# Slots 4 and 5 interleaved by the halves of w, one piece of w settled on another engine, and new engine orders for slots 0 to 25

## The chip, the cores and the metric

One core of a Trainium2 chip runs the whole kernel. The metric is the time of one execution in device microseconds. A profiled execution gives a page and a trace besides; its times are microseconds from the start of its span.

## The reference

```python
xw = x @ w                                   # x: 16 x 2048 x 1024, w: 1024 x 1024
out[:, 0, :] = xw[:, 0, :]
for t in range(1, S):                        # S = 2048
    out[:, t, :] = decay[None, :] * out[:, t - 1, :] + xw[:, t, :]
```

A dense matrix product, and behind it a first-order recurrence along time, of its own decay for each of the 1024 columns.

## The kernel before

**Tiles and slots.** Time is cut into 64 chunks of 512 steps, and two chunks of one batch make a group. The 1024 output columns are cut into 8 parts n of 128. One tile is a group by a part: 128 columns on the partitions, 1024 steps along the free side. TensorE works tile by tile in *slots*: slot s is the s-th tile, so slots 0 to 7 are chunks 0 and 1, slots 8 to 15 are chunks 2 and 3, and so on. A tile takes 16 matmuls of 512 columns (8 blocks k of w's rows by two chunks). Slots 0 to 3 are computed together, with their chunks in pieces, while x and w still arrive; slots 8 and 9 are also computed together.

**How x comes.** Each chunk is read by four DMAs (`load`, L105) of 256 KB that GpSimd issues and that turn float32 into bfloat16, into one of three buffers `xb`. VectorE transposes the chunk in 32x32 blocks into one of two buffers `xw` (`turn`, L115, called T), and ScalarE copies that in two halves into one of five buffers `xt` (`part`, L123, called X and Y), which TensorE reads. When T of chunk c is recorded, the four loads of chunk c+3 join a list; each L in an order takes the next load from that list.

**How w comes.** w lies in four staging quarters: half h of the columns by even or odd rows e. `settle` (L326) turns one piece m of a quarter into bfloat16 in `wsb`. Pieces are numbered i = 8h + 4e + m, so pieces 8 to 11 are the third quarter (even rows of the second half of the columns, which slots 4 to 7 need) and 12 to 15 the fourth (its odd rows). `W` settles on VectorE and `w` on ScalarE. `r` makes GpSimd copy one element of a settled piece (L376), so that what stands behind it on GpSimd waits for that piece.

**The recurrence.** Tiles whose n is 3 or 7 are scanned by VectorE out of PSUM (S at L229). The others are *paired*: ScalarE copies the tile out of PSUM (p, L191) and multiplies the even steps by the decay (g, L171); GpSimd adds these to the odd steps (j, L205); VectorE scans the odd steps alone, half as many (S at L210); ScalarE multiplies (h, L171) and GpSimd adds (c, L266) to fill in the even steps. z sets the element before the first (L199, L201) and k keeps the last (L270). `flips` turns the kind of some tiles over: tile 1 is scanned whole, so is tile 13. At last VectorE transposes a tile back (B, L278) into one of four buffers `ot`; when four tiles are there, SyncE issues four DMAs of 512 KB to the output (L302).

**PSUM.** Tiles rotate over three buffers `ps`. Slot 4 takes that of tile 0, slot 5 that of tile 1, and, farther on, slot 22 that of tile 19 and slot 26 that of tile 23. TensorE may start a tile only when the tile before it in the buffer has been read: by p and g where it is paired, by S where it is not.

**What sets the order.** Nothing is scheduled by the compiler: `pin` keeps the order in which the code records instructions, engine by engine. A table by hand, `agenda`, lists for each slot what is recorded behind its matmuls, for slots 0 to 33 and the last 20; the slots between follow the rule `usual`. An order says nothing of when: each engine runs its own list in order, waiting by semaphores for what it needs. Only the order within one engine counts, so a deed may stand under a later slot and still come at the same place of its engine's list.

Of the kernel before, what the change touches and what calls it, by code (L numbers as in the profile page):

```python
# [10 lines left out]
BF16 = mybir.dt.bfloat16  # L11
# [14 lines left out]
def kernel(  # L26
# [34 lines left out]
    K = CQ // P  # L61
    M = K // 2
    TL = 512
    NJ = TL // P
    NC = S // TL
    R = K // 2
# [3 lines left out]
    const = ctx.enter_context(tc.tile_pool(name="const", bufs=1))  # L70
    sb = ctx.enter_context(tc.tile_pool(name="sb", bufs=1))
    psp = ctx.enter_context(tc.tile_pool(name="psp", bufs=1, space=bass.MemoryType.PSUM))
# [3 lines left out]
    def ring(pool, name, count, shape, dtype=FP32):  # L76
        i = turns[name] = turns.get(name, -1) + 1
        return pool.tile(shape, dtype, name=f"{name}{i % count}")
# [20 lines left out]
    xt_of = {}  # L99
# [25 lines left out]
    def matmul(ps, n, k, xt, t0=0, t1=TL, start=0, pairs=None):  # L125
        if pairs is None:
            rhs = xt[:, k // 2, k % 2, t0:t1]
        else:
            rhs = pairs[:, k // 2, t0 // P:t1 // P, :, k % 2].rearrange("p j i -> p (j i)")
        lhs = wsb[:, k, n].rearrange("p q i -> p (q i)")  # L130
        return pin(nc.tensor.matmul(  # L131
            out=ps[:, t0 % ps.shape[1]:][:, 0:t1 - t0],
            lhsT=lhs,
            rhs=rhs,
            start=(k == 0 and t0 == start),
            stop=(k == K - 1),
        ))
# [233 lines left out]
        settle(i // 8, i // 4 % 2, i % 4, copy)  # L371

    def await_settled(i):
        mark = const.tile([128, 1], BF16, name="mark")
        h, e, m = i // 8, i // 4 % 2, i % 4
        pin(nc.gpsimd.tensor_copy(out=mark, in_=wsb[:, 2 * m + e, h * R, 0, 0:1]))  # L376

# [35 lines left out]
    def finale():  # L413
        six, six_late = ring(psp, "ps", 3, [128, TL]), ring(psp, "ps", 3, [128, TL])
        seven, seven_late = ring(psp, "spare", 1, [128, TL]), ring(psp, "ps", 3, [128, 2 * TL])
        return ((six[:, 0:TL // 2], six_late[:, TL // 2:TL]),
                (seven[:, 0:TL // 2], (seven_late[:, 0:TL // 4], seven_late[:, TL:TL * 5 // 4])))

    def half_of(n, half, ks=range(K)):
        ps = finals[n % R - 2][half]  # L420
        t = half * (TL // 2)
        for k in ks:
            matmul(ps, n, k, xt_of[nch - 1], t, t + TL // 2, t)
# [60 lines left out]
    def turn_and_load(c):  # L484
# [42 lines left out]
    }  # L527
    agenda = {
        -99: "M0 U0 M1 M2 M3 U1 U2 w0 W1 w2 W3 K3 E0 E1 G0 E2 G1 E3 F2 G3 W4 w5 W6 W7 D E4 E5 G4 E6 G5 E7 F6 G7 E8 E9 G8 E10 G9 E11 F10 G11 E12 L E13 G12 L E14 G13 E15 L F14 G15",
        0: "p0 z0",  # L530
        1: "g0 S1 w8 w9 w10 w11",
        2: "L L",
        3: "p2 z2 L W12 W13 W14 W15 g2 r15 j0 S3 k1",
        4: "j2 B1 d k3 L L",
        5: "p4 S0 g4 S2 k0 h0 j4 L L B3 h2",
        6: "k2 c0 T2 c2 L p5 g5 B0 L X2 L",
        7: "B2 L L Y2 T3 L z4 z5 j5 p6 S4 z6 L g6 L X3 S5 j6 S7 Y3 L S6 h4 k7 k5 c4 k4 h5 B7",
        8: "",
        9: "k6 h6 c5 B4",
        10: "p8 g8 c6 T4 z8 p9 j8 g9 B5 X4",  # L540
        11: "L j9 B6 p10 S8 L z9 z10 g10 S9 h8",
        12: "j10 Y4 S11 L c8 h9 T5 c9",
        13: "p12 L g12 B9 j12 X5 S10 L",
        14: "Y5 B8 L B11 h10 z12 c10 S13",
        15: "p14 L g14 S12 j14 T6 h12 L",
        16: "p15 c12 g15 B10 L X6 j15 B12",
        17: "z14 Y6 S14 L B13 z15 h14 S15 p16 z16 c14",
        18: "g16 T7 L h15 j16 p17 g17 B14 z17 c15 X7",
        19: "S16 j17 p18 B15 L g18 L S17 k16 h16 z18 j18",
        20: "Y7 S19 L c16 k17 h17 T8 k19 L c17",  # L550
        21: "p20 g20 L S18 X8 j20 B17 B19",
        22: "L h18 p21 c18 B16 k18 g21 B18 Y8 z20 L j21 S20",
        23: "p22 z21 z22 S21 L h20 g22 T9 c20 h21",
        24: "k21 k20 j22 S23 X9 L c21 Y9 B20 L",
        25: "B23 k23 p24 B21 g24 z24 j24 S22 z25",
        26: "p25 T10 k22 h22 g25 c22 S24 X10 j25",
        27: "B22 p26 S25 g26 z26 Y10 j26",
        28: "S27 h25 h24 c25 S26 c24",
# [36 lines left out]
    def usual(s):  # L595
        paired = [t.paired for t in tiles]
        do = [f"P{s}"] if paired[s] else []
        if paired[s - 1]:
            do.append(f"S{s - 1}")
        if not paired[s]:  # L600
            do.append(f"S{s}")
        do.append(f"C{s - 1}")
        if paired[s - 2]:
            do.append(f"B{s - 2}")
        if not paired[s - 1]:
            do.append(f"B{s - 1}")
        return do + later.get(s, []) + ["L"] * (2 if len(loads) > NQ else 1)
# [8 lines left out]
    def perform(do):  # L616
        for deed in do:
            deeds[deed[0]](int(deed[1:] or 0))
# [3 lines left out]
    for step, (g, n) in enumerate(slots):  # L622
        T = TL * len(g)
        left = step - len(slots)
        if n % R == 0:
            ns, nj = range(n, n + R), T // P
            if left == -2 * R:
                outlets = [Outlet(ns, H, half) for half in range(2)]
            else:
                pieces = 1 if left < -7 * R else 2 if left < -6 * R else nj // H  # L630
                outlets = [Outlet(ns, nj, pieces=pieces)]
        if left == -R:
            outlets = []
        if step == 0:
            heads = [ring(psp, "ps", 3, [128, T]) for _ in range(3)]
            firsts = [ps[:, 0:TL] for ps in heads] + [spares[0]]
            seconds = [ps[:, TL:T] for ps in heads] + [spares[1]]
            for j0, j1 in cuts[0]:
                for e in range(2):
                    for k in range(e, K, 2):  # L640
                        for i in range(R):
                            matmul(firsts[i], i, k, xt_of[0], j0 * P, j1 * P, j0 * P,
                                   pairs=None if e else xw_of[0])
            Q = cuts[1][0][1] * P
            for k0 in range(0, K, 2):
                for i in range(R):
                    for k in (k0, k0 + 1):
                        matmul(seconds[i], i, k, xt_of[1], 0, Q,
                               pairs=xw_of[1] if k0 < 4 else None)
            for i in range(R):  # L650
                for k in range(K):
                    matmul(seconds[i], i, k, xt_of[1], Q, TL, Q,
                           pairs=xw_of[1] if i < 2 else None)
        if step < R:
            ps = heads[n] if n < 3 else tuple(spares)
        else:
            if step == K + 1:
                ps = nexts
            elif left >= -2:
                finals = finals if left == -1 else finale()  # L660
                ps = finals[left + 2]
            elif len(g) == 2 or n % R < 3:
                ps = ring(psp, "ps", 3, [128, T])
            else:
                ps = ring(psp, "spare", 1, [128, TL])
            todo = [(k, l) for k in range(K) for l in range(len(g))]
            if step < K:
                todo.sort(key=lambda kl: kl[0] % 2)
            elif step == K:
                todo = []  # L670
                nexts = (ring(psp, "spare", 1, [128, TL]), ring(psp, "ps", 3, [128, T])[:, TL:T])
                for l in range(len(g)):
                    for i, one in enumerate((ps[:, l * TL:(l + 1) * TL], nexts[l])):
                        for k in range(K):
                            matmul(one, n + i, k, xt_of.get(g[l]),
                                   pairs=xw_of[g[l]] if l or not i and k >= M else None)
            elif step == K + 1:
                todo = []
            if left == -2:
                for m, half in ((n, 0), (n + 1, 0), (n, 1)):  # L680
                    half_of(m, half)
            if left >= -2:
                todo = []
            if 40 <= step < 180:
                pin(nc.tensor.nop(hint="room", nofuse=True))
            for k, l in todo:
                matmul(ps[:, l * TL:(l + 1) * TL], n, k, xt_of[g[l]])
        tiles.append(Tile(g, n, ps, outlets))
        do = agenda.get(step, agenda.get(left) if left >= -20 else None)
        if do is None:  # L690
            do = usual(step)
        else:
            do = do.split()
            if left == -20:
                do = rest(step) + do
        perform(do)
# [29 lines left out]
```

## Time and profile before

| | |
|---|---|
| median of 3 runs (lowest, highest) | 903.59 us (903.53, 903.96) |
| the profiled execution's own time | 905.63 us |
| its span | 903.8 us |
| TensorE busy | 890.3 us, 99% |
| VectorE, ScalarE, GpSimd busy | 825.1, 686.1, 656.5 us |
| granted TensorE clock, mean of the core | 1.0 |
| DMA | 204.77 MB, mean 227 GB/s |

The profiled execution is 1.8 us longer than its span, and 2.0 us over the median of the runs without a profile. Busy time of TensorE is modelled from matmuls that overlap: a matmul of 512 columns is shown with some 0.38 us, while starts lie 0.216 us apart. A few per cent of the matmul records are missing.

### The profile page before, as it was taken

Reading aid. Unit: us, or ns where it says so; the run is one execution under the profiler, and the core shown is the slowest. Engines: PE = TensorE matmul, PEld = TensorE weight load, DVE = VectorE, ACT = ScalarE, POOL = GpSimd, SP = SyncE. Lnnn points to the kernel's source line nnn. Section 1 sums busy time; section 2 is a strip of 40 time slices with the busy share of each in tenths; the row PEclk is TensorE's granted clock in tenths of the full one; section 3 lists DMA queues with packets and bytes.
Section 4 is the critical chain, followed back from the end, with each engine's and each line's share of the span. In section 5 each row is a group of like instructions: output and inputs, shape, how many; then the busy total and the mean of one; then the engine's idle time right before and its main releaser. Section 6 shows DMA issues by size and latency. Waiting matters only on the chain.

```text
span 903.8 us, 12213 instructions
## 1 busy us (share of the span) xinstructions
PE 890.3 (99%) x4130; PEld 412.7 (46%) x4211; DVE 825.1 (91%) x632; ACT 686.1 (76%) x958; POOL 656.5 (73%) x757
## 2 busy tenths in 40 slices
PE   7999999999999999999999999999999999999997
PEld 5544444444444444444444444444444444444444
DVE  4999998998999999999998999999999999999998
ACT  3899968877877877778778778777787787787743
POOL 7978679777767777777677687777777776876632
PEclk9999999999999999999999999999999999999999
DMA  9999999999999999999999999999999999999868
GB/s 185 176 215 215 219 245 213 215 231 255 249 245 257 254 253 249 251 247 234 224 233 228 223 232 226 233 225 227 231 231 226 229 236 222 226 228 215 180 148 229
DMA packets 403182, 204.77 MB, mean 227 GB/s; under 512 B 9392, under 2 KB 402096, under 8 KB 403120
## 3 DMA queue, kind: packets, MB, share of 16 engines
q1 hardware_dynamic: 265808, 134.77, 61.0%
q0 software_dynamic: 137024, 68.70, 56.3%
q8 instruction: 33, 0.54, 0.2%
q10 hardware_dynamic: 288, 0.52, 0.2%
q14 instruction: 29, 0.24, 0.1%
HBM read 138.42 MB, written 134.22 MB: 302 GB/s over the span
## 4 chain that ended last, share of the span: by engine, by line
PE 97%; DMA 1%; issue 1%; POOL 0%; DVE 0%; DVEq 0%; POOLq 0%
PE ps L131 96%; DMA xb<-in_x_dram 1%; PE spare L131 1%; POOL xb L105 0%; PE spare L410 0%; PE ps L410 0%; DVE h L438 0%; DVE xw L115 0%; DVEq L721 0%; DVEq L115 0%; POOLq L710 0%
## 5 line engine op out<-in xcount | busy, mean ns | idle before, releaser
L131 PE MATMUL ps<-xt,wsb 128*128 128x512 bf16 (+1 forms) x3959 | 861.6, 377 | 4.3
L131 PEld LDWEIGHTS <-wsb 128*128 128x128 bf16 x4184 | 408.2, 98 | 477.8 <-issue 1.0
L205 POOL TENSOR_TENSOR xs<-h,xs 128x512 f32<-128x512 f32 (+1 forms) x190 | 242.6, 1277 | 187.5 <-ACT h L171 84.8
L278 DVE STREAM_TRANSPOSE ot<-so 128x1024 f32<-128x1024 f32 (+2 forms) x264 | 300.4, 1176 | 5.1 <-DMA out_dram<-ot 2.5
L191 ACT COPY xs<-ps 128x1024 f32<-128x1024 f32 (+1 forms) x190 | 188.9, 994 | 152.1 <-PE ps L131 140.7
L266 POOL TENSOR_TENSOR so<-h,xs 128x512 f32<-128x512 f32 (+1 forms) x189 | 240.5, 1274 | 41.7 <-ACT h L171 25.7
L123 ACT COPY xt<-xw 128x2048 bf16<-128x2048 bf16 (+3 forms) x136 | 242.3, 1790 | 8.2 <-DVE xw L115 8.2
L105 POOL DMA_DIRECT2D xb<-in_x_dram x264 | 173.8, 659 | 5.2 <-DMA xb<-in_x_dram 3.6
L171 ACT ACTIVATE h<-so,dec 128x512 f32<-128x512 f32 (+1 forms) x189 | 144.8, 767 | 27.9 <-DVE so L210 24.6
L115 DVE STREAM_TRANSPOSE xw<-xb 128x2048 f32<-128x2048 f32 (+3 forms) x78 | 147.3, 1900 | 7.5 <-DMA xb<-in_x_dram 7.5
L210 DVE TENSOR_TENSOR_SCAN so<-spare,keep,xs 128x512 f32<-128x512 f32 (+1 forms) x97 | 119.8, 1238 | 26.4 <-POOL xs L205 26.2
L210 DVE TENSOR_TENSOR_SCAN so<-spare,xs 128x512 f32<-128x512 f32 x93 | 113.3, 1219 | 25.6 <-POOL xs L205 22.7
L171 ACT ACTIVATE h<-ps,dec 128x512 f32<-128x512 f32 (+1 forms) x190 | 129.9, 684 | 0.0
L229 DVE TENSOR_TENSOR_SCAN so<-dec,ps 128x1024 f32<-128x1024 f32 x34 | 76.9, 2262 | 2.4 <-PE ps L131 1.6
L229 DVE TENSOR_TENSOR_SCAN so<-dec,keep,ps 128x1024 f32<-128x1024 f32 (+2 forms) x35 | 75.4, 2154 | 0.0
L270 ACT COPY keep<-so 128x1 f32<-128x1 f32 x136 | 25.5, 190 | 9.1 <-DVE so L229 8.7
L201 ACT COPY so<-keep 128x1 f32<-128x1 f32 x97 | 18.5, 191 | 2.5 <-DVE ot L278 2.3
L131 PE MATMUL ps<-xw,wsb 128*128 128x256 bf16 (+3 forms) x72 | 12.2, 306 | 0.6 <-DVE xw L115 0.6
L131 PE MATMUL spare<-xt,wsb 128*128 128x512 bf16 (+3 forms) x60 | 12.6, 329 | 0.0
L199 POOL MEMSET so<- 128x1 f32 x93 | 10.7, 116 | 0.6 <-DVE ot L278 0.6
L345 PE MATMUL spare<-wide,seed 128*128 128x512 f32 x10 | 7.3, 905 | 3.2 <-ACT seed L338 3.2
L319 POOL DMA_DIRECT2D ot<-in_w_dram x12 | 6.5, 544 | 1.8 <-DMA xb<-in_x_dram 0.9
(43 smaller groups left out, 38.0 us busy)
## 6 DMA issues: line engine op xcount, KB each, us to landing
out_dram<-ot SPq DMA_DIRECT2D x236, 512.0 KB, 10.8
xb<-in_x_dram POOLq DMA_DIRECT2D x248, 256.0 KB, 7.8
out_dram<-ot SPq DMA_DIRECT2D x56, 128.0 KB, 2.7
out_dram<-ot SPq DMA_DIRECT2D x8, 256.0 KB, 4.5
ot<-in_w_dram POOLq DMA_DIRECT2D x12, 128.0 KB, 5.2
xb<-in_x_dram POOLq DMA_DIRECT2D x8, 128.0 KB, 5.5
out_dram<-xb SPq DMA_DIRECT2D x3, 256.0 KB
xb<-in_x_dram POOLq DMA_DIRECT2D x4, 160.0 KB, 7.4
```

Source lines behind the costliest of these rows:

```text
L105: pin(nc.gpsimd.dma_start(out=xb_of[c][quad(q), j0:j1], in_=_ap(x, [[D, P], [P * D, j1 - j0], [1, CQ]], (b * S + t0 + j0 * P) * D + q * CQ)))
L115: pin(nc.vector.transpose(out=dst.rearrange("p (m j i) -> p j m i", m=M, i=P)[:, j0:j1, m0:m1], in_=src.rearrange("p (j m c) -> p j m c", ...
L123: pin(copy(out=xt_of[c][:, m0:m1, :, j0 * P:j1 * P], in_=src))
L131: return pin(nc.tensor.matmul(out=ps[:, t0 % ps.shape[1]:][:, 0:t1 - t0], lhsT=lhs, rhs=rhs, start=(k == 0 and t0 == start), stop=(k == K ...
L171: pin(nc.scalar.activation(out=h[:, i * size:(i + 1) * size], in_=src, func=mybir.ActivationFunctionType.Copy, scale=dec[:, self.n:self.n ...
L191: pin(nc.scalar.copy(out=self.xs[:, i * size:(i + 1) * size], in_=ps))
L205: pin(nc.gpsimd.tensor_tensor(out=odds, in0=self.g, in1=odds, op=ALU.add))
L210: pin(nc.vector.tensor_tensor_scan(out=so[:, 3:T + 2:2], data0=squares[-1][:, n:n + 1].to_broadcast([128, T // 2]), data1=self.xs[:, 1:T:2 ...
L229: return pin(nc.vector.tensor_tensor_scan(out=so[:, t + 2:t + 2 + size], data0=dec[:, n:n + 1].to_broadcast([128, size]), data1=ps, initia ...
L266: pin(nc.gpsimd.tensor_tensor(out=self.so[:, 2:T + 2:2], in0=self.h, in1=self.xs[:, 0:T:2], op=ALU.add))
L270: pin(nc.scalar.copy(out=self.keep, in_=self.so[:, self.T + 1:self.T + 2]))
L278: pin(nc.vector.transpose(out=outlet.ot[:, :, c0:c0 + P], in_=self.so[:, 2 + t0:2 + t0 + nj * P].rearrange("p (i t) -> p i t", t=P)))
```

## The change

The 32 matmuls of slots 4 and 5 are recorded in a new order. Before, slot 4's even row blocks, slot 4's odd ones, slot 5's even ones, slot 5's odd ones; after, slot 4 even, slot 5 even, slot 4 odd, slot 5 odd. Piece 8 of w is settled by VectorE instead of ScalarE, as the first thing behind slots 0 to 3's inputs. A second `r` (r8) makes GpSimd wait for that piece, beside the one for piece 15, and each has an element of its own to write. The agenda of slots 0 to 25 is rewritten; it holds the same deeds otherwise. From slot 26 on nothing is changed.

```diff
-        mark = const.tile([128, 1], BF16, name="mark")
+        mark = const.tile([128, 1], BF16, name=f"mark{i}")
...
-        0: "p0 z0",
-        1: "g0 S1 w8 w9 w10 w11",
-        2: "L L",
-        3: "p2 z2 L W12 W13 W14 W15 g2 r15 j0 S3 k1",
-        4: "j2 B1 d k3 L L",
-        5: "p4 S0 g4 S2 k0 h0 j4 L L B3 h2",
-        6: "k2 c0 T2 c2 L p5 g5 B0 L X2 L",
-        7: "B2 L L Y2 T3 L z4 z5 j5 p6 S4 z6 L g6 L X3 S5 j6 S7 Y3 L S6 h4 k7 k5 c4 k4 h5 B7",
-        8: "",
-        9: "k6 h6 c5 B4",
-        10: "p8 g8 c6 T4 z8 p9 j8 g9 B5 X4",
-        11: "L j9 B6 p10 S8 L z9 z10 g10 S9 h8",
...
-        17: "z14 Y6 S14 L B13 z15 h14 S15 p16 z16 c14",
-        18: "g16 T7 L h15 j16 p17 g17 B14 z17 c15 X7",
-        19: "S16 j17 p18 B15 L g18 L S17 k16 h16 z18 j18",
-        20: "Y7 S19 L c16 k17 h17 T8 k19 L c17",
-        21: "p20 g20 L S18 X8 j20 B17 B19",
-        22: "L h18 p21 c18 B16 k18 g21 B18 Y8 z20 L j21 S20",
-        23: "p22 z21 z22 S21 L h20 g22 T9 c20 h21",
-        24: "k21 k20 j22 S23 X9 L c21 Y9 B20 L",
-        25: "B23 k23 p24 B21 g24 z24 j24 S22 z25",
+        0: "",
+        1: "",
+        2: "",
+        3: "W8 L p0 g0 w9 S1 w10 W12 W13 W14 W15 w11 r8 z2 p2 k1 L g2 L S3 d r15 j0 B1 j2 S0 L k3 L",
+        4: "",
+        5: "z0 p4 L g4 S2 h0 T2 B3 h2",
+        6: "c0 k0 B0 p5 c2 g5 z5 j4 X2 T3 p6 j5 Y2 S4 L g6",
+        7: "L X3 L S5 S7 k2 L L z4 L h4 j6 c4 B2",
         8: "",
+        9: "Y3 B7 k7 p8 S6 z6",
+        10: "L g8 h5",
+        11: "c5 h6 B4 j8 T4 k5 k4 c6 p9 S8 z8 g9 p10 h8 g10 L j9 X4 L k6 B5 L B6 z10",
...
+        17: "g15 z15 j14 j15 p16 T6 B12 g16 S14 L X6 S15 h14 Y6 T7 j16 c14 h15 S16",
+        18: "L p17 g17 c15 p18 B13 B15 z16 h16",
+        19: "j17 k16 z17 L c16 g18 L B14 Y7 S17",
+        20: "j18 L h17 L S19 z18",
+        21: "X7 T8 p20 g20 k19 k17 L S18 L c17 j20 B16 X8 p21 L z20 L L B17",
+        22: "g21 h18 Y8 S20 j21 c18 h20",
+        23: "p22 z21 k18 T9 S21 g22 c20 h21 Y9 B19",
+        24: "",
+        25: "p24 B18 g24 S23 k21 B20 k20 X9 k23 j22 c21 B21 z24 B23 L L z22 j24 z25 S22",
...
             if step == K + 1:
                 ps = nexts
+            elif step == R + 1:
+                ps = fives
...
-            if step < K:
+            if step == R:
+                todo = []
+                fives = ring(psp, "ps", 3, [128, T])
+                for e in range(2):
+                    for i, one in enumerate((ps, fives)):
+                        for k in range(e, K, 2):
+                            for l in range(len(g)):
+                                matmul(one[:, l * TL:(l + 1) * TL], n + i, k, xt_of[g[l]])
+            elif step == R + 1:
+                todo = []
+            elif step < K:
                 todo.sort(key=lambda kl: kl[0] % 2)
```

The rows of slots 12 to 16 are left out here; they too are rewritten.

## The prediction

> **What bounds the kernel now.** I read the page first, then TensorE's waits, then the transfers of the stretch that the new orders cover, then VectorE and GpSimd there, in order of time. The page's first line and TensorE's list of waits:
>
> ```profile
> PE 890.3 (99%) x4130; PEld 412.7 (46%) x4211; DVE 825.1 (91%) x632; ACT 686.1 (76%) x958; POOL 656.5 (73%) x757
> ```
> ```profile
> PE spare L345 <- ACT seed L338: 3.2, 1, 3.2
> PE spare L345 <- ACT gate L361: 0.8, 1, 0.8
> PE ps L131 <- DVE xw L115: 0.6, 1, 0.6
> ```
>
> TensorE waits three times, the last time at 19.58 us, before slot 4, and the diff touches nothing ahead of slot 4. From there on the starts of its matmuls lie 0.216 us apart (0.227 where they read `xw`), and gaps are whole multiples of 0.216, which are missing records. So the changed stretch has no wait to remove: the change can gain about nothing, and costs whatever wait it brings. Behind TensorE stand the transfers. Their view from 57 to 111 us:
>
> ```profile
> GB/s 216 214 214 216 215 214 216 214 215 214 215 219 212 216 214 215 214 215 215 214 215 215 214 215 216 215 215 214 216 215 214 219 212 215 215 215 215 214 215 215
> q0 software_dynamic: 11561, 5.74, 76.9%
> q1 hardware_dynamic: 11561, 5.83, 52.7%
> out_dram<-ot SPq DMA_DIRECT2D x12, 512.0 KB, 18.2
> xb<-in_x_dram POOLq DMA_DIRECT2D x19, 256.0 KB, 12.9
> ```
>
> Flat at 215 GB/s, half of it loads: 5.74 MB in 54 us are 21.9 loads of 262,144 bytes, one each 2.46 us, and the landing events stand 2.46 us apart from 52.4 to 111.5 us. Here loads can't be hurried; a gap in their queue is not made good. VectorE in the same stretch, and GpSimd before it:
>
> ```profile
> 89.31 4.59 DVE L278 STREAM_TRANSPOSE ot<-so 128x1024 f32<-128x1024 f32 x4
> 93.82 2.49 DVE L210 TENSOR_TENSOR_SCAN so<-spare,xs 128x512 f32<-128x512 f32 x2
> 96.22 2.29 DVE L115 STREAM_TRANSPOSE xw<-xb 128x2048 f32<-128x2048 f32 x1
> 98.43 2.25 DVE L229 TENSOR_TENSOR_SCAN so<-dec,ps 128x1024 f32<-128x1024 f32 x1
> ```
> ```profile
> 41.59 1.31 POOL L205 TENSOR_TENSOR xs<-h,xs 128x512 f32<-128x512 f32 x1
> 42.84 0.10 POOL L199 MEMSET so<- 128x1 f32 x1
> 42.88 1.30 POOL L105 DMA_DIRECT2D xb<-in_x_dram  x2
> ```
>
> The turn at 96.22 is T9, the scan behind it S23, which frees the PSUM of slot 26; it ends at 100.68. Slot 26 starts at 47.62 (slot 10) + 16 x 3.453 = 102.87, so S23 has 2.2 us to spare. VectorE has no wait from 60 us to here: chunk 9 landed at 94.23, before its turn. The issue at 42.88 is the first load of chunk 6.
>
> **The change part by part.**
>
> *Slots 4 and 5.* The same 32 matmuls: 0. Odd pieces of w are needed at 26.70 + 16 x 0.216 = 30.15 instead of 28.42; they are there from 27.62 to 28.23 now, so no wait goes. Tile 5's PSUM is needed at 28.42 instead of 30.15; S1, which frees it, ends at 27.44: hidden by 1.0 us. Tile 4 is whole after 24 matmuls, at 31.9 instead of 30.15; tile 5 at 33.6 as before.
>
> *Piece 8.* On VectorE a piece costs 0.20 us, on ScalarE 0.52. Its quarter lands at 24.28, VectorE has done it by 24.6, and S1 starts at 25.15 as now, since TensorE releases it: 0, at worst 0.3 if that cover were gone. ScalarE's three other pieces are ready 0.52 earlier. r8 is one copy on GpSimd (0.19 us), waiting to about 24.65; the loads of chunk 3 behind it were issued at 25.66 and aren't later.
>
> *Early deadlines* (starts by the ScalarE chain below): X2 ends at 39.1, needed at 40.51; Y2 at 41.8, needed at 43.1. No wait, with 1.3 us in hand.
>
> *Chunk 6's first load.* This is where I find the price. In the new order of GpSimd this load stands behind c0, c2, j4, j5, j6, c4, c5, j8 and c6. By rows of the waits before (start to start): p 0.90, g 0.58, h 0.68 (0.78 when its end is waited for), X or Y 1.80, k 0.09, j or c 1.25. p4 starts at 32.1; p4, g4, h0 end at 34.4; c0 ends at 35.65, and p5, which reuses its buffer, starts at 35.7. From there ScalarE runs p5 g5 X2 p6 Y2 g6 X3 k2 h4 Y3 k7 p8 g8 h5 without a wait: 0.90 + 0.58 + 1.80 + 0.90 + 1.80 + 0.58 + 1.80 + 0.09 + 0.68 + 1.80 + 0.09 + 0.90 + 0.58 + 0.78 = 13.3, so h5 ends at 49.0. Then GpSimd's c5, j8, c6 take 3.75: the load is issued at 52.75 instead of 42.88. Chunk 5's last load lands at about 54 to 55, so the queue runs dry. What a load costs from issue to landing in a dry queue is shown by two answers, without stores (28 to 40 us) and with them (195 to 260 us):
>
> ```profile
> xb<-in_x_dram POOLq DMA_DIRECT2D x8, 256.0 KB, 6.4
> ```
> ```profile
> xb<-in_x_dram POOLq DMA_DIRECT2D x19, 256.0 KB, 7.8
> ```
>
> The least in the second stretch is 7.1. Stores run from 46 us in the new order, so I take 7.5: landing at 60.25 instead of 57.33. Bounds: 4.6 (the shortest without stores) and 8.6 (the longest with them).
>
> The Trainium skill (DMA: Bandwidth & Descriptors, Anatomy of one DMA — SWDGE (gpsimd) path) gives such a DMA about 2.0 us fixed plus its bytes at 436 GB/s, by which 256 KB would be an estimated 2.6 us, the load would follow chunk 5 at once, and the sum below would be 0. The rows above say otherwise.
>
> *From there to TensorE.* Chunk 7 is complete 7 x 2.46 later, at 77.5, and VectorE, there at 75.4, waits for it at T7. Behind it stand S16, three B, S17, S19, T8, S18, two B, S20: 2.20 + 1.12 + 3.38 + 1.12 + 2.20 + 2.20 + 1.12 + 2.25 + 1.12 = 16.7, so T9 is reached at 94.2. Chunk 9 is complete at 60.25 + 15 x 2.46 = 97.15: VectorE waits 3 us. Behind T9 now stand S21, B19 and B18 ahead of S23: 97.2 + 2.2 + 1.12 + 2.25 + 2.25 = 105.05. TensorE, due at 102.87, waits 2.2 us; with the signals 2.3. Queued behind T9 on VectorE are also the back transposes of tiles 20 to 23, whose stores have buffers to spare; and behind slot 26 everything is TensorE's and shifts with it. Nothing gives the 2.3 us back, since TensorE has no other wait.
>
> With the bounds of the latency the wait is 0 to 3.4. ScalarE's p26, p28 and p30 follow with little in hand once VectorE is late (I count some 0.2 to 0.3 us): none to 0.5 us more; I take none.
>
> **Sum.** The profiled execution would have a span of 903.8 + 2.3 = 906.1 and a time of 907.9; the runs without a profile lie 2.0 lower, so the median goes from 903.59 to 905.9 us, 0.26% up. About 0.2% (1.8 us) is what a measurement of this kernel can tell from no change.
>
> **Rivals.**
>
> *The load comes in time: no change (0.31).* The place is chunk 6's first load, the price 0 to 1.7 us, so 903.6 to 905.3. It decides at a landing of 59.7: if the load is issued before 52.2 or its latency is under 7.0, the wait falls under 1.8; at 57.9 or sooner it is nil, since T9 is then reached at about the time its chunk lands. For it: the issue time is a sum of some twenty durations, and the margin is 0.5 us; without stores 4.6 to 6.6 us were seen in a short queue. Against it: with stores, no row is under 7.1.
>
> *A gain (0.03).* TensorE would have to lose a wait of 1.8 us behind slot 4, and has none. Only the start-up differs from run to run; 901.5 would need that.
>
> *The wait cools the clock (0.04).* TensorE's first spin matmuls start 0.853 us apart for 5.3 us and then 0.43 apart: the array starts at half speed. A wait of 0.8 us at 11.3 was followed at full speed; none of 2.3 us is in the trace. If 2.3 us halved the clock for 5.3 us again, 12 matmuls would take 5.3 us instead of 2.65: 2.65 more, 908.5. The Trainium skill (TensorE: Matmul & The Clock Gate, What's actually happening) says that a whole idle window of about 3.4 us brings the half clock back; by that rule 2.3 us does not, and a second mishap is needed.
>
> *The orders change nothing on the engines:* excluded, the two programs' instruction lists differ engine by engine as told.
>
> **How the numbers follow.** Likeliest: slower by the 2.3 us wait, 905.9, with its own range 905.4 to 907.5; 0.62; with the clock's case slower in all 0.66, no change 0.31, faster 0.03. The range runs from 903.4 (load in time) to 908.5 (the clock).
>
> **What would show it.** In the changed kernel's profile: a line PE ps L131 <- DVE so L229 of 2 to 2.5 us near 102.9, once; waits of VectorE's turns for `xb` at about 75 and 94; the first load of chunk 6 issued near 52.8, landing near 60.3, and the loads behind it 2.46 apart to 114; no wait of TensorE from 19.6 to 100. I am wrong if TensorE has no wait, if it waits elsewhere (slots 8 to 10 for X2 or Y2, or behind slot 26 for ScalarE), or if loads run faster than one in 2.46 us.

## The result

| | before | after |
|---|---|---|
| median (lowest to highest, 6 runs each) | 903.78 us (903.53 to 904.34) | 907.73 us (907.45 to 908.55) |
| ratio of the runs, 95% interval | 1 | 1.0044 (1.0032 to 1.0057) |
| profiled execution, its own time / span | 905.63 / 903.8 us | 907.71 / 905.9 us |
| granted TensorE clock, mean of the core | 1.0 | 0.998 in all six runs |

The change makes the kernel 0.44% slower, 3.95 us. TensorE's busy time and its list of waits in the changed kernel (total, times, longest):

```profile
PE 896.1 (99%) x4211; PEld 412.9 (46%) x4211; DVE 825.7 (91%) x633; ACT 686.1 (76%) x957; POOL 657.0 (73%) x758
```
```profile
PE spare L345 <- ACT seed L338: 3.2, 1, 3.2
PE ps L131 <- DVE so L229: 2.9, 1, 2.9
```

The second wait is the new one: once, for a scan of VectorE out of PSUM. (A busy sum of 896.1 instead of 890.3 says little: here no matmul record is missing, before 81 were.) The timeline of VectorE around it shows whose wait it passes on, and TensorE's shows where it ends:

```profile
76.59 2.31 DVE L115 STREAM_TRANSPOSE xw<-xb 128x2048 f32<-128x2048 f32 x1 [2.40 <-DMA xb<-in_x_dram]
...
96.27 2.31 DVE L115 STREAM_TRANSPOSE xw<-xb 128x2048 f32<-128x2048 f32 x1 [2.91 <-DMA xb<-in_x_dram]
98.50 1.19 DVE L210 TENSOR_TENSOR_SCAN so<-spare,xs 128x512 f32<-128x512 f32 x1
99.61 2.33 DVE L278 STREAM_TRANSPOSE ot<-so 128x1024 f32<-128x1024 f32 x2
101.87 2.25 DVE L229 TENSOR_TENSOR_SCAN so<-dec,ps 128x1024 f32<-128x1024 f32 x1
```
```profile
104.17 36.16 PE L131 MATMUL ps<-xt,wsb 128*128 128x512 bf16 x159 [2.85 <-DVE so L229]
```

The two turns are T7 and T9, each behind an idle stretch that a load ended. Behind T9 stand S21, two back transposes (B19, B18) and only then S23, which ends at 104.12; slot 26 starts at 104.17. Before, the same T9 began at 96.22 with nothing to wait for, and S23 stood right behind it. (The two times look alike because slot 4 begins at 24.98 in this profile and at 26.70 in that of before: counted from slot 4, T9 is 1.8 us later.) GpSimd's timeline shows where the load of chunk 6 now stands, behind c5, j8 and c6:

```profile
47.36 1.30 POOL L266 TENSOR_TENSOR so<-h,xs 128x512 f32<-128x512 f32 x1 [1.55 <-ACT h L171]
48.63 1.29 POOL L205 TENSOR_TENSOR xs<-h,xs 128x512 f32<-128x512 f32 x1
49.88 1.28 POOL L266 TENSOR_TENSOR so<-h,xs 128x512 f32<-128x512 f32 x1
51.11 0.67 POOL L105 DMA_DIRECT2D xb<-in_x_dram  x1
```

By the trace's landing events this load takes 7.31 us, and it lands 4.95 us behind the one before it, where 2.46 is the rule of the stretch: the stream of loads lost 2.5 us. At the issue the load before it was still under way (it landed at 53.47), and yet the queue ran dry: from 53.13 to 54.79 the trace has packets of the stores' queue alone, and the first of the load queue behind that start 3.7 us after the issue.

One thing more happens behind the wait. Activity by windows, cut into stretches of 3.41 us; the columns are PE, PEld, DVE, ACT and POOL busy (instructions), then the granted clock:

```profile
97.86:101.28 3.42, 3.42 (x17) 1.46 (x15) 3.42 (x4) 1.47 (x2) 1.20 (x2) 1.00 1.29 212
101.28:104.69 3.41, 0.56 (x4) 0.28 (x3) 3.41 (x3) 3.41 (x6) 2.70 (x5) 1.00 1.30 215
104.69:108.10 3.41, 3.41 (x10) 1.23 (x9) 3.41 (x4) 2.43 (x5) 0.61 (x1) 0.50 1.30 214
108.10:111.51 3.41, 3.41 (x18) 1.51 (x16) 3.41 (x3) 2.10 (x4) 1.91 (x2) 1.00 1.30 215
```

In the stretch that follows the wait the clock is half. Seven starts of matmuls in it lie 0.427 us apart instead of 0.216, and one at each edge 0.33 and 0.31: 1.69 us more in all.

So the time went to two terms. Counted by the starts of matmuls (the idle time that the views print is a little shorter, since a matmul is drawn longer than the distance of two starts), slot 26 begins 3.02 us late, and the half clock adds 1.69: 4.71 us. From the start of slot 4's first matmul to that of the last matmul of L131 the profile has 876.08 us against 871.38 before: 4.70 more. No other loss shows on TensorE.

### The profile page after: what moved, and what is told of

It is laid out like the page before. It is cut to its first block, busy times and chain, and to the rows that moved or that the text cites. A ratio compares the mean times of both kernels' runs of the same rounds, so it can differ in the third digit from the quotient of the medians.

```text
span 905.9 us, 12298 instructions
## 1 busy us (share of the span) xinstructions
PE 896.1 (99%) x4211; PEld 412.9 (46%) x4211; DVE 825.7 (91%) x633; ACT 686.1 (76%) x957; POOL 657.0 (73%) x758
## 4 chain that ended last, share of the span: by engine, by line
PE 91%; DMA 3%; ACT 2%; POOL 2%; issue 1%; DVE 1%; ACTq 0%; DVEq 0%
PE ps L131 89%; DMA xb<-in_x_dram 2%; DMA out_dram<-ot 2%; PE spare L131 1%; PE spare L345 1%; POOL so L266 1%; ACT h L171 1%; ACT xt L123 1%; ACT xs L191 0%; DVE so L229 0%; POOL xs L205 0%; POOL xb L105 0%; DVE so L210 0%; DVE ot L278 0%; ACT L338 0%
## 5 line engine op out<-in xcount | busy, mean ns | idle before, releaser
L131 PE MATMUL ps<-xt,wsb 128*128 128x512 bf16 (+2 forms) x4040 | 867.7, 377 | 2.9 <-DVE so L229 2.9
L131 PEld LDWEIGHTS <-wsb 128*128 128x128 bf16 x4184 | 408.4, 98 | 481.8 <-issue 5.8
L131 PE MATMUL spare<-xt,wsb 128*128 128x512 bf16 (+3 forms) x60 | 12.6, 329 | 0.0
L131 PE MATMUL ps<-xw,wsb 128*128 128x256 bf16 (+3 forms) x72 | 12.2, 306 | 0.0
```

The lines of the kernel that those rows point to most:

```text
L131: return pin(nc.tensor.matmul(out=ps[:, t0 % ps.shape[1]:][:, 0:t1 - t0], lhsT=lhs, rhs=rhs, start=(k == 0 and t0 == start), stop=(k == K ...
```

## The experiments

Theory A: the first loads of chunk 6 are issued late, the load queue runs dry and never makes it good, VectorE waits at T9, and what now stands between T9 and S23 hands that wait to TensorE; the half clock comes on top as a consequence. Rivals: the new order of VectorE makes the wait by itself; the order of slots 4 and 5, piece 8 and r8 cost something; the half clock costs nothing that the wait had not cost already. The runs were made in three sets, each beside the kernel before. Its median was 904.01 us (33 runs) for the kernel without the new orders, S23 closer, chunk 6 early and the wait filled; 903.82 (27) for both chunks early, the repeated kernel before and the two with late loads; 903.68 (21) for the wait filled in part, VectorE's order alone and both cures. Gains and losses below are against these; where nothing else is said there were 11 runs.

**Only what is not an order of engines.** Slots 4 and 5 interleaved, piece 8 on VectorE, r8, all with the old agenda:

```diff
-        0: "p0 z0",
-        1: "g0 S1 w8 w9 w10 w11",
-        3: "p2 z2 L W12 W13 W14 W15 g2 r15 j0 S3 k1",
+        0: "W8 p0 z0",
+        1: "g0 S1 w9 w10 w11",
+        3: "p2 z2 L W12 W13 W14 W15 g2 r8 r15 j0 S3 k1",
```

> The kernel before with the matmul order of slots 4 and 5, piece 8 on VectorE and the second wait of GpSimd on it, but the old engine orders. Theory A: these parts cost nothing by themselves in slots 22 to 27; tile 4 is whole 1.7 us later, so in the old order of ScalarE p4 delays p5 and X2, and slot 8 may wait some 0.5 us: 903.5 to 904.6. Rival (the matmul order is what costs): 906 or more.

Measured: 904.31 us, ratio 1.0001 (0.9992 to 1.0010). TensorE waits 0.4 us once for a copy of x at 39.65, and S23 not at all. These parts cost nothing that can be measured; the loss lies in the orders.

**S23 closer behind T9.** The changed kernel with B19 put into VectorE's wait ahead of T9, and B18 behind S23:

```diff
-        23: "p22 z21 k18 T9 S21 g22 c20 h21 Y9 B19",
-        25: "p24 B18 g24 S23 k21 ...
+        23: "p22 z21 k18 B19 T9 S21 g22 c20 h21 Y9",
+        25: "p24 g24 S23 B18 k21 ...
```

> The new kernel with one thing moved on VectorE: back transpose 19 goes ahead of T9, into VectorE's 2.9 us wait for chunk 9, and back transpose 18 goes behind S23. The loads are as late as in the new kernel. Theory A (late loads and the two transposes ahead of S23 make the wait together, and the wait halves TensorE's clock for 3.4 us): S23 starts 2.25 us sooner, TensorE's wait falls from 2.85 to about 0.6 us and the clock stays whole, so 2.25 + 1.7 = about 3.9 us are won back and the median is 904 to 904.7; ScalarE may bring a further wait of a few tenths. Rival (the late loads alone cost what they are late, some 3 us): the wait stays over 2 us, 906 or more. Rival (the matmul order of slots 4 and 5 costs): 907.7.

Measured: 905.02 us, ratio 1.0010 (1.0001 to 1.0019), a little above the range of theory A. Its TensorE waits behind slot 4:

```profile
PE ps L131 <- DVE so L229: 0.9, 1, 0.9
PE ps L131 <- ACT h L171: 0.6, 1, 0.6
```

T9 still begins only when its chunk has landed, at 96.59, but S23 ends at 102.18, and the wait falls from 2.9 to 0.9 us. The clock stays whole. A new wait of 0.6 us for ScalarE's `h` comes at 113. The order between T9 and S23 is thus one half of the cause: it passes the wait on.

**Chunk 6 early.** The changed kernel with the four loads of chunk 6 right behind chunk 5's:

```diff
-        10: "L g8 h5",
-        11: "... h8 g10 L j9 X4 L k6 B5 L B6 z10",
-        13: "c9 L p12 ...
+        10: "L L L L L g8 h5",
+        11: "... h8 g10 j9 X4 k6 B5 B6 z10",
+        13: "c9 p12 ...
```

> The new kernel with the four loads of chunk 6 issued directly behind chunk 5's, ahead of c5 on GpSimd, and nothing else moved. Theory A: the load queue does not run dry, chunk 9 is complete some 2.3 us sooner (93.6 instead of 95.9), S23 ends 2.3 us sooner, TensorE's wait falls from 2.85 to 0.6 us or nothing and the clock stays whole: 903.6 to 904.6. Rival (the order on VectorE alone, two transposes ahead of S23, costs 2.25 us whatever the loads do): wait still about 2.3 us, 906 or more. Rival (matmul order): 907.7.

Measured: 905.37 us, ratio 1.0013 (1.0004 to 1.0022), above what was expected. The wait for S23 is 2.0 us, not gone:

```profile
PE ps L131 <- DVE so L229: 2.0, 1, 2.0
```
```profile
45.73 2.58 POOL L105 DMA_DIRECT2D xb<-in_x_dram  x4
48.58 0.65 POOL L105 DMA_DIRECT2D xb<-in_x_dram  x1 [0.28 <-issue]
59.61 1.30 POOL L105 DMA_DIRECT2D xb<-in_x_dram  x2
```

Five loads are now issued by 49.2, and then GpSimd has none for 10.4 us. By the landing events the load issued at 59.6 landed 4.10 us behind the one before it: the queue ran dry one chunk later instead, although two loads were still to land at that issue (at 60.87 and 63.30). The experiment had moved the hole, not filled it. What it did settle is the clock: with 2.0 us of waiting it stayed whole in all eleven runs.

**Both chunks early.** The same, and the first two loads of chunk 7 moved up as well:

```diff
-        11: "... h8 g10 L j9 X4 L k6 B5 L B6 z10",
-        13: "c9 L p12 S11 T5 g12 L L B9 ...
+        11: "... h8 g10 j9 L L X4 k6 B5 B6 z10",
+        13: "c9 p12 S11 T5 g12 B9 ...
```

> The new kernel with the four loads of chunk 6 behind chunk 5's and, as well, the first two of chunk 7 issued behind j9, some 5 us sooner: in the run with chunk 6's loads alone the queue ran dry again at chunk 7 (67.1 where 65.4 was possible) and TensorE still waited 2.2 us. Theory A: chunk 9 is complete at about 93.4 instead of 95.1, TensorE's wait falls from 2.2 to about 0.5 us: 903.5 to 904.2. Rival (the order on VectorE costs 2.2 us whatever the loads do): 905.4 as in that run.

Measured: 903.79 us, ratio 0.9997 (0.9989 to 1.0006). The loss is gone, with VectorE's new order left as it was. The loads of chunks 6 to 9 land some 2.46 us apart again but for one, T9 begins at 94.22 instead of 96.27, and the wait for S23 is 0.6 us. The argument rests on this experiment above all: the late loads are the root, and with the loads in time the order costs nothing that the medians show.

**The wait filled.** The changed kernel with 14 extra matmuls of 512 columns into a free bank ahead of slot 26, 14 x 0.216 = 3.0 us of work that the result does not use:

```diff
+            if step == 26:
+                fill = ring(psp, "spare", 1, [128, TL])
+                for _ in range(14):
+                    pin(nc.tensor.matmul(
+                        out=fill, lhsT=wsb[:, 0, 0].rearrange("p q i -> p (q i)"),
+                        rhs=xt_of[g[0]][:, 0, 0, 0:TL], start=True, stop=True))
```

> The new kernel with 14 further matmuls of 512 columns (3.0 us) into the free PSUM bank between slots 25 and 26, so that TensorE computes while it would wait for S23; their result is read by nobody. Theory A with the clock: the wait of 2.85 us is replaced by 3.0 us of work, the clock stays whole, and the 1.7 us of the half clock are won back: about 906.2, 1.5 us under the new kernel. Rival (the half clock costs nothing, the wait alone is the loss): 907.7 to 907.9.

Measured: 906.40 us, ratio 1.0023 (1.0014 to 1.0032), and the clock whole. TensorE is held back for about as long as by the wait, yet the loss is 2.39 us instead of 3.95: 1.56 less, near the 1.69 that the slow matmuls came to. So the half clock was a cost of its own.

**The wait filled in part.** The same with two matmuls:

> The changed kernel with two extra 512-column matmuls (0.43 us) into a free bank ahead of slot 26: they do no work of the result and shorten TensorE's idle stretch from 2.85 to about 2.4 us. If idleness between 2.2 and 2.4 us is still too short to halve the clock: clock whole, 906.0 to 906.5 us. If the clock falls all the same: 907.5 to 908 us, half clock for 3.4 us in the record.

Measured: 907.98 us (4 runs), ratio 1.0042 (1.0029 to 1.0056). In three of the four runs the mean clock is 0.997 or 0.998, at 907.68 to 908.36 us; in the fourth it is 1.0, at 906.42. The idle stretch in the profile is 2.40 us and still halved the clock:

```profile
100.66:104.08 3.42, 1.25 (x6) 0.49 (x5) 3.42 (x3) 3.42 (x7) 2.65 (x4) 1.00 1.30 215
104.08:107.49 3.41, 3.18 (x8) 1.16 (x8) 3.41 (x4) 3.02 (x7) 1.30 (x1) 0.50 1.30 215
```

**From the other side: the kernel before, unchanged and made worse step by step.** First the kernel before once more:

> The kernel before, unchanged, profiled once more. Looked at is what lies outside the stretch from slot 4's first matmul to the last: in the five profiles of changed kernels it is 29.8 to 30.2 us of the span, in the one profile of the kernel before 32.4 us. If that profile was only a slow start, this one shows 30.0 to 31 us, a span near 902.2 and 904.0 us, and 871.4 us in between without a wait. If the kernel before starts slower for a reason of its own, it shows 32 us again.

Measured: 903.92 us, ratio 1.0000 (0.9991 to 1.0009); profiled 904.06 us, span 902.3. Slot 4 begins at 25.61 in it, and at 26.70 in the profile that the prediction was made from: the first profile had a start-up 1.1 us longer, and 0.7 us more behind the last matmul. In between the repeated one has 871.65 us instead of 871.38: two small gaps, of 0.06 us at 50.05 and of 0.22 ahead of slot 16.

Then chunk 6's first three loads late, as in the changed kernel:

```diff
-        7: "... j5 p6 S4 z6 L g6 L X3 S5 j6 S7 Y3 L S6 ...
-        10: "p8 g8 c6 T4 z8 p9 j8 g9 B5 X4",
+        7: "... j5 p6 S4 z6 g6 X3 S5 j6 S7 Y3 S6 ...
+        10: "p8 g8 c6 T4 z8 p9 j8 L L L g9 B5 X4",
```

> The kernel before with one part of the new orders: the first three loads of chunk 6 are issued behind c6 and j8 on GpSimd, some 9 us later than now, so that the load queue runs dry for about 2.5 us. VectorE's order is the old one, S23 directly behind T9. Theory A: chunk 9 is complete 2 to 3 us later, T9 waits under 1 us, S23 still ends in time for slot 26, and TensorE has no wait there (at most some 0.5 us elsewhere, near slot 16): 903.8 to 904.7. Rival (late loads alone cost what they are late): 906 or more.

Measured: 905.04 us, ratio 1.0011 (1.0002 to 1.0019), a little above the range. Chunk 9's last load lands at 95.72, 1.9 us later than in the repeated profile of before, but T9 doesn't wait for it: VectorE itself is late by then, and T9 begins at 96.25 (95.58 in the repeated profile). S23 ends at 100.71 and makes no wait. The loss is elsewhere, at slot 16: four loads in a row, three of them moved there, hold GpSimd for 2.58 us ahead of the add that a scan waits for, and S13 comes late.

```profile
51.48 2.58 POOL L105 DMA_DIRECT2D xb<-in_x_dram  x4
54.06 1.32 POOL L205 TENSOR_TENSOR xs<-h,xs 128x512 f32<-128x512 f32 x1
```
```profile
55.41 1.28 DVE L210 TENSOR_TENSOR_SCAN so<-spare,keep,xs 128x512 f32<-128x512 f32 x1 [0.73 <-POOL xs L205]
...
65.61 2.30 DVE L229 TENSOR_TENSOR_SCAN so<-dec,keep,ps 128x1024 f32<-128x1024 f32 x1
```
```profile
67.97 72.25 PE L131 MATMUL ps<-xt,wsb 128*128 128x512 bf16 x334 [0.87 <-DVE so L229]
```

The edit brought a wait of its own, so its time says less than its profile: late loads alone do not reach TensorE at slot 26. Nor would they without the loss at slot 16: in the kernel with no wait (the last one below) slot 26 starts 76.18 us behind slot 4, which would be 101.43 here, 0.7 us after S23's end.

Then VectorE's new order alone, S21, B19 and B18 between T9 and S23, with the loads where they were:

```diff
-        21: "p20 g20 L S18 X8 j20 B17 B19",
-        22: "L h18 p21 c18 B16 k18 g21 B18 Y8 z20 L j21 S20",
-        23: "p22 z21 z22 S21 L h20 g22 T9 c20 h21",
+        21: "p20 g20 L S18 X8 j20 B17",
+        22: "L h18 p21 c18 B16 k18 g21 Y8 z20 L j21 S20",
+        23: "p22 z21 z22 L h20 g22 T9 S21 c20 h21 B19 B18",
```

> The kernel before with VectorE's S21, B19 and B18 between T9 and S23, as the changed kernel has them, and the loads of chunk 6 where they were. Theory A (the late loads of chunks 6 and 7 make the wait, the order behind T9 only passes it on): chunk 9 is complete at its old time, 93.7 to 94.2 us, VectorE waits at T9 for some 2 us instead of doing those pieces, S23 ends near 102.3, before slot 26 is due (102.7): no TensorE wait for S23 above 0.4 us, 903.8 to 904.3 us. Rival B (VectorE's order by itself makes the wait): TensorE waits 2 to 3 us for S23, 905.9 to 907 us.

Measured: 904.72 us, ratio 1.0011 (1.0002 to 1.0020). The time is above what theory A said; the place agrees with it. VectorE waits 1.97 us at T9, which begins at 93.71, S23 ends at 101.56, and slot 26 begins within 0.1 us of when it is due. What TensorE loses, 1.2 us by its starts, comes behind that:

```profile
109.04 3.61 PE L131 MATMUL ps<-xt,wsb 128*128 128x512 bf16 x16 [0.36 <-ACT h L171]
113.20 27.14 PE L131 MATMUL ps<-xt,wsb 128*128 128x512 bf16 x125 [0.55 <-ACT h L171]
```

ScalarE's `z` waits 2.77 us there for the back transposes that the edit moved, and its `p` and `h` come late; the changed kernel's own order of ScalarE avoids that. (The profiled run was the highest of the eleven, 906.65 us, and has one more wait, of 1.7 us near 158, for a load that came late; I take that for this run's own.)

Last both together:

> The kernel before with the late loads of the run above and, on VectorE, S21 and back transposes 19 and 18 put between T9 and S23 as in the new kernel; nothing else of the change. Theory A: T9 starts when chunk 9 is complete, S23 3.4 us later than without, and TensorE waits 1 to 2 us at slot 26, short enough to leave the clock whole: 905.2 to 906.3. Rival (something else of the change makes the wait): no wait at slot 26, 904.7 or less.

Measured: 907.15 us (5 runs), ratio 1.0032 (1.0020 to 1.0045), above the range, with the clock whole. T9 begins at 96.11 behind 2.28 us of waiting, S23 ends at 103.96. By its starts TensorE loses 1.08 us at slot 16, 0.44 at slot 26, and 1.23 for `h` behind it: 2.75; five small gaps before 51 us make another 0.5. Slot 26 was already 1.08 late by the loss at slot 16, so S23 came 1.5 us behind the time at which slot 26 would have been due. Late loads alone gave 0 there, the order alone 0.1: only the two together reach TensorE at slot 26.

**Both cures.** The changed kernel with both chunks' loads early, and with B19 ahead of T9 and B18 behind S23 (the edits of the second and the fourth experiment):

> The changed kernel with the loads of chunks 6 and 7 early and with B19 ahead of T9 and B18 behind S23. Theory A: the two cures meet the same wait, so the second adds only what is left after the first (0.6 us of waiting for S23): no wait for S23, 903.2 to 903.9 us. Rival: moving B18 behind S23 keeps its output buffer for longer and brings the waits for ScalarE's h that the kernel with B19 first showed (0.6 us): 903.9 to 904.6 us.

Measured: 903.44 us (903.16 to 903.91), ratio 0.9998 (0.9989 to 1.0006). TensorE waits for nothing behind slot 4: VectorE waits only 0.31 us at T9, and S23 ends at 99.63.

```profile
94.03 2.31 DVE L115 STREAM_TRANSPOSE xw<-xb 128x2048 f32<-128x2048 f32 x1 [0.31 <-DMA xb<-in_x_dram]
96.26 1.19 DVE L210 TENSOR_TENSOR_SCAN so<-spare,xs 128x512 f32<-128x512 f32 x1
97.37 2.26 DVE L229 TENSOR_TENSOR_SCAN so<-dec,ps 128x1024 f32<-128x1024 f32 x1
```

It beats the changed kernel by some 4 us, and cannot be told from the kernel before.

## Why the prediction was right, and where its size was off

**What bounds the kernel: right.** TensorE runs without a wait from slot 4 on, and the change could only add one. The cured version, with no wait at all, ends where the kernel before does.

**Parts at nothing: right.** Slots 4 and 5, piece 8 and r8 with the old orders came to a ratio of 1.0001. No wait for X2 or Y2 shows in the changed kernel.

**Chunk 6's first load: right, once the start-up is taken off.** Forecast: issued at 52.75, landing at 60.25. Measured: 51.11 and 58.42. Slot 4 began at 24.98 in this profile instead of 26.70; counted from there the issue is at 26.13 against a forecast 26.05, and the landing at 33.44 against 33.55. The sum of some twenty durations along ScalarE's chain was good to 0.1 us, and the latency taken, 7.5, is 7.31 in the trace. The estimate of 2.6 us from the Trainium skill (DMA: Bandwidth & Descriptors, Anatomy of one DMA — SWDGE (gpsimd) path) does not hold in this stretch, in which stores run beside the loads; the kernel with both chunks early shows what a load in time means, no loss in the median. One reading of the working was wrong: the longest latency from 195 to 260 us is 9.0, not 8.6. With it the wait's upper bound would have been 3.8 us instead of 3.4.

**From there to TensorE: right in mechanism, 0.7 us short in size.** Counted from slot 4, T9 was to start at 70.45 and did at 71.29; S23 was to end at 78.35 and did at 79.14; slot 26 was due at 76.17 as forecast (76.18). (The last addends of the forecast come to 105.02, not 105.05.) The term that was too small is the load rate: fifteen landings behind the first, at 2.46 us each with one exception. The third load of chunk 7 landed 3.29 us behind the one before it, 0.83 more than the rule. The kernels with early loads show the same step at the next load (3.41 to 3.81 us), and so does the kernel before with late loads (3.73 at the third load of chunk 7, but the load behind it lands after 1.88); the kernel with late loads and VectorE's order doesn't (2.50). What makes it stays open. The step turned a wait of 2.3 us into 3.02 by the starts.

**The clock: the rival at 0.04 came true beside the likeliest case.** The prediction took the half clock for a separate mishap and left it out of the sum. It was a consequence of the wait, in all six runs: half clock for 3.41 us in the profile, 1.7 us lost. Of the forecast 2.65 us it is less, since the slow stretch lasted 3.41 us and not 5.3. The Trainium skill's condition (TensorE: Matmul & The Clock Gate, What's actually happening), a whole idle window of about 3.4 us, was the argument for the low chance; the trace contradicts it, with 0.56 us of matmuls in the 3.41 us stretch. That 907.73 lies inside the forecast range was in part luck: it is above the likeliest case's own range (905.4 to 907.5), and the whole range reaches beyond it only through this rival.

**The sum.** Forecast 2.3 us, measured 3.95 in the median. The two terms give 4.71; the rest can be placed against the repeated profile of before: slot 4 begins 0.63 us earlier in the changed kernel (24.98 against 25.61), slot 4 to the last matmul is 4.43 longer, the tail is 0.18 shorter, together 3.62, beside 3.65 in the two executions' own times. Slot 4 begins at 24.95 to 25.36 in the eight profiles with the interleaved slots 4 and 5, at 25.25 to 25.74 in the four of the old order that were taken with the experiments. The medians point the same way: in the eight kernels with the interleaved slots they lose 0.2 to 1.2 us less than the starts of their profiles show from slot 4 on, in the three others that were changed between 0.2 more and 0.3 less (without the late wait near 158). So the change seems to gain some tenths at the start; what makes that was not tested.

**ScalarE's later steps: none taken, none found** in the changed kernel. They came, 0.7 to 1.2 us by the starts, in three of the four experiments that moved a back transpose.

## What to carry to other kernels

In a transfer queue that is always full, as this one, the place of a single issue had no price until the queue ran dry once: then the whole stream was late by the gap, and a consumer many steps on paid. When an order by hand moves an issue, work out when it is issued and how long what is queued by then will last. One load still under way was too little here, since the new load's first packets came 3.7 us after its issue; in the kernel with chunk 6 early even two were. And look at what stands between the late consumer and the engine that sets the end; one of the two may be harmless without the other. A wait on TensorE may cost more than its length, when the clock falls behind it.

## What the runs showed of the hardware that was not expected

**The clock is decided in windows of a fixed raster.** In the changed kernel's record of the granted clock the whole-speed periods are 95.573 us and, after the half-speed stretch of 3.413 us, 798.719 us: 28 and 234 times 3.413. In the kernel with two fillers all three are the same numbers; in the kernel before and the others without a fall in mid-kernel the whole-speed period is 894.292 or 897.705, 262 or 263 times 3.413. So the decision falls at multiples of 3.413 us from the time that the clock first rose; that it is about the window just ended, and not about the wait's length alone, the figures below bear out. The Trainium skill (TensorE: Matmul & The Clock Gate, What's actually happening) gives a free-running window of 4096 cycles, 3413 ns, and the traces agree with this part of it.

What the runs add is how idle a window has to be. With 0.56 us busy of 3.41 (the changed kernel) and with 1.25 (two fillers) the clock fell. In the kernel with chunk 6 early a wait of 2.0 us lay across a boundary, and it did not:

```profile
98.84:102.25 3.41, 2.58 (x12) 1.08 (x11) 3.41 (x4) 3.15 (x3) 2.31 (x3) 1.00 1.30 215
102.25:105.67 3.42, 2.21 (x11) 1.03 (x11) 3.42 (x4) 3.06 (x7) 1.64 (x3) 1.00 1.30 215
105.67:109.08 3.41, 3.41 (x18) 1.52 (x17) 3.41 (x3) 2.25 (x5) 0.20 (x1) 1.00 1.30 215
```

The kernel with VectorE's order alone narrows it. Its wait of 1.7 us near 158 fell into one window of its raster (8.10 + 44 x 3.4133 = 158.29), left 1.79 us busy, and the clock stayed whole:

```profile
158.29:161.70 3.41, 1.79 (x9) 0.83 (x9) 3.41 (x3) 3.41 (x7) 3.39 (x4) 1.00 1.30 214
161.70:165.11 3.41, 3.41 (x18) 1.52 (x17) 3.41 (x4) 2.81 (x5) 2.14 (x3) 1.00 1.31 214
```

Between 1.25 and 1.79 us busy of 3.41 the bound is open. In all thirteen traces, the idle ends of the kernels included, every window behind the first rise with 1.25 us or less was followed by half clock, and every one with 1.79 or more by the whole. By this the place of a wait in the raster counts, and a wait of 2.4 us could cool the clock in some runs and not in others, as it did in three of four; that this is why the fourth was spared is not shown, since only one of the four was profiled.

**A load into a queue that runs dry beside stores took 6.6 to 7.8 us.** It took 7.31 us in the changed kernel, 7.79 in the one with chunk 6 early, 6.75 and 6.55 in the two kernels with late loads, for the same 256 KB that land 2.46 us apart while the queue is full. Half of it and more passed before the load's first packets: 3.7 us in the changed kernel and the two with late loads, 4.7 in the one with chunk 6 early.
